# Expert feed-forward of a two-block transformer on one core: the four weight chunks of a group are loaded in reverse, and the group's matmuls are issued as one run

## The chip, the cores and the metric

The kernel runs on one core of one Trainium2 chip. The metric is the device time of one execution in microseconds. Three runs of the kernel before took 2832.05, 2836.18 and 2837.74 us; their median is 2836.18 us.

## What is computed

The reference runs two transformer blocks after each other over 512 tokens of width 1024, with a context of 256 tokens beside them. The first block mixes tokens by retention, window attention and neighbourhood attention, and ends in a feed-forward with 16 experts. This is the part that the change touches (`expert_choice_ffn`): each expert chooses its 64 best tokens by the router's probabilities, and computes for them, in float32,

```python
h = silu(xe @ w_gate[e]) * (xe @ w_up[e])     # [64, 1024] x [1024, 1024], twice
y = (h @ w_down[e]) * prob[e]                 # [64, 1024] x [1024, 1024]
out = out.at[idx[e]].add(y)
```

The second block is two layers of latent attention, pooling and a gated linear attention. Its work on the context (`ctx2`) needs nothing of the first block, and so can run at the same time as the experts.

## The kernel before

The kernel is written as Python generators. Each yields an estimate of the time that it has just written down, and `weave(main, fill, ratio)` takes one piece of the main work and then as many pieces of the fill as that estimate buys. In the experts' stage the main work is `experts` and the fill is `ctx2` of the second block's first layer, with a ratio of 0.8. What is written so is then put in order, engine by engine, by a list scheduler: of the instructions that are ready by its own estimates it takes the one of the highest priority, which is by default the place in the text. The order that results is fixed when the kernel is built, and each engine runs its list in order.

The 16 experts are taken in 8 pairs `p`. One pair has 24 weight pieces of 256 rows, `chunk(p, i, h)` being one half of such a piece: 128 partitions by 1024 float32, 512 KB, into a buffer `we`, loaded by SP's queue (line 1296). The first 44 chunks go to 20 buffers of an early pool (`NEARLY`, `NPRE`), all later ones to 8 buffers (`s.nbig`). A `group` is four chunks, `e` in 0, 1 (the expert of the pair) by `h` in 0, 1. It makes eight matmuls (line 1306): in `h`, in `kk`, and then the two experts. The tokens of an expert (64 columns of `xe`, or of `hT`) are stationary, 512 weight columns stream, and expert 0 writes partitions 0 to 63 and expert 1 partitions 64 to 127 of one PSUM tile. So the two matmuls of an `e` pair use different column halves of the array. Two groups give one PSUM tile (`G`, `U` or `Yp`); `act` makes the gated product from `G` and `U` by ACT and DVE (lines 1337 to 1339), `hturn` transposes it (line 1345), `Yp` is scaled by ACT (line 1374) and added to the result in DRAM by POOL's indirect DMAs (line 1380). An expert pair has 12 groups, the stage 96.

The fill's projections load a 128x1024 piece of weights (`wr`, line 412, SP's queue too, two buffers), split it into a high and a low part (`wh` by ACT at line 395, `wl` by DVE at line 391, three buffers each), and make three matmuls for each product (lines 404, 405, 406). In the trace each float32 matmul of line 1306 appears as two records, so a group is 16 records and a pair of matmuls four.

Of the kernel before, what the change touches and what calls it, by code (L numbers as in the profile page):

```python
# [10 lines left out]
AF = mybir.ActivationFunctionType  # L11
ALU = mybir.AluOpType
# [305 lines left out]
class Kern:  # L318
# [967 lines left out]
    def experts(s):  # L1286
        nc = s.nc
        wx = s.d["wexp"]

        def chunk(p, i, h):  # L1290
            if s.pre:
                s.pre -= 1
                w = s.early.tile([128, 1024], F32, name=s.uid("we"), tag="early", bufs=NEARLY)
            else:
                w = s.big.tile([128, 1024], F32, name=s.uid("we"), tag="wbig", bufs=s.nbig)
            nc.sync.dma_start(w, wx[p, i][:, h * 1024:h * 1024 + 1024])
            return w

        def group(p, c0, stat, ps, kh):

            for h in range(2):
                ws = [chunk(p, c0 + e, h) for e in range(2)]
                for kk in range(2):
                    k = 4 * kh + 2 * h + kk
                    for e in range(2):
                        nc.tensor.matmul(ps[64 * e:64 * e + 64, :], stat[:, k, 64 * e:64 * e + 64],  # L1306
                                         ws[e][:, kk * 512:kk * 512 + 512], start=k == 0, stop=k == 7)

        def gather(p):
            xg = s.T(nm="xg", tag="u")  # L1310
            nc.gpsimd.indirect_dma_start(out=xg, out_offset=None, in_=s.h2d, in_offset=bass.IndirectOffsetOnAxis(
                ap=s.idx128[:, p:p + 1], axis=0))
            return xg

        def turn(xg):
            xe = s.T(nm="xe", tag="u").rearrange("p (k n) -> p k n", k=8)
            for g in range(2):
                pt = s.at()
                for j in range(4):
                    k = 4 * g + j  # L1320
                    nc.tensor.transpose(pt[:, j * 128:j * 128 + 128], xg[:, k * 128:k * 128 + 128], s.const("ident"))
                (nc.scalar.copy if g else nc.vector.tensor_copy)(
                    xe[:, 4 * g:4 * g + 4, :], pt.rearrange("p (j n) -> p j n", j=4))
            return xe

        xg = gather(0)
        xe = turn(xg)
        for p in range(8):
            if p < 7:
                xg = gather(p + 1)  # L1330
            hT = s.T(nm="hT", tag="u").rearrange("p (k n) -> p k n", k=8)
            eth = s.T(nm="eth", tag="u")
            hd = []

            def act(f, G, U):
                th = eth[:, f * 512:f * 512 + 512]
                nc.scalar.activation(th, G, AF.Tanh, scale=0.5)
                nc.vector.scalar_tensor_tensor(th, th, 1.0, G, ALU.add, ALU.mult)
                nc.vector.tensor_tensor(th, th, U, ALU.mult)
                hd.append(th)  # L1340

            def hturn(f):
                pt = s.at()
                for j in range(4):
                    nc.tensor.transpose(pt[:, j * 128:j * 128 + 128], hd[f][:, j * 128:j * 128 + 128], s.const("ident"))
                nc.scalar.copy(hT[:, 4 * f:4 * f + 4, :], pt.rearrange("p (j n) -> p j n", j=4))  # L1346

            for f in range(2):
                G = s.mm()
                for kh in range(2):  # L1350
                    group(p, 8 * f + 2 * kh, xe, G, kh)
                    yield 3.6
                U = s.mm()
                for kh in range(2):
                    group(p, 8 * f + 4 + 2 * kh, xe, U, kh)
                    yield 3.6
                act(f, G, U)
                if f == 1:
                    if p < 7:
                        xe = turn(xg)  # L1360
                    hturn(0)
                    yield 1.4
            if p == 7:
                s.sums()
            ye = s.T(nm="ye", tag="u") if p < 7 else s.T(F32R, "ye", "u")
            for o in range(2):
                Yp = s.mm()
                for kh in range(2):
                    if o == 0 and kh == 1:
                        hturn(1)  # L1370
                    group(p, 16 + 4 * o + 2 * kh, hT, Yp, kh)
                    yield 3.6
                yo = ye[:, o * 512:o * 512 + 512]
                nc.scalar.activation(yo, Yp, AF.Copy, scale=s.gate[:, p:p + 1])
                if p == 7:
                    yl = s.T(F32R, "yl", "pj5")
                    nc.vector.scalar_tensor_tensor(yl, Yp, s.gate[:, p:p + 1], yo.bitcast(F32), ALU.mult, ALU.subtract)
                    s.last += [(yo[:, j * 128:j * 128 + 128], yl[:, j * 128:j * 128 + 128]) for j in range(4)]
            for e in range(2 if p < 7 else 0):
                nc.gpsimd.indirect_dma_start(  # L1380
                    out=s.ffd, out_offset=bass.IndirectOffsetOnAxis(ap=s.idx64[0:64, 2 * p + e:2 * p + e + 1], axis=0),
                    in_=ye[64 * e:64 * e + 64, :], in_offset=None, compute_op=ALU.add)
# [728 lines left out]

PACE = (2, 2.5, 2.5)
NEARLY = 20
NPRE = 44
LATE = True
XF = 1.0, 1.0
# [26 lines left out]
def body(tc, d, out):  # L2143
    from contextlib import ExitStack
    with ExitStack() as ctx:
# [16 lines left out]
        fill = Fill()  # L2162
        k.nbig, k.pre = 8, NPRE
        big = ExitStack()
# [49 lines left out]
```

## Time and profile before

| | |
|---|---|
| median of three runs | 2836.18 us |
| the profiled execution, its own time | 2832.7 us |
| its span | 2830.9 us |
| TensorE, matmuls (PE) busy | 2691.5 us, 95% |
| TensorE, weight loads (PEld) busy | 1867.8 us, 66% |
| VectorE (DVE) busy | 1567.8 us, 55% |
| ScalarE (ACT) busy | 1230.2 us, 43% |
| GpSimd (POOL) busy | 159.9 us, 6% |
| HBM read and written | 484.06 MB and 48.76 MB |
| first to last matmul of the experts | 828.6 to 1581 us of the span |

The time outside the span is 2832.7 - 2830.9 = 1.8 us. The page gives for each engine its busy time, then the span in 40 slices of about 71 us. The experts' stage is slices 12 to 22 of these. A busy PE in these tables has an instruction in its pipeline; how fast matmuls follow each other is read from their start times in the timeline.

### The profile page before, as it was taken

Reading aid. Unit: us, or ns where it says so; the run is one execution under the profiler, and the core shown is the slowest. Engines: PE = TensorE matmul, PEld = TensorE weight load, DVE = VectorE, ACT = ScalarE, POOL = GpSimd, SP = SyncE. Lnnn points to the kernel's source line nnn. Section 1 sums busy time; section 2 is a strip of 40 time slices with the busy share of each in tenths; the row PEclk is TensorE's granted clock in tenths of the full one; section 3 lists DMA queues with packets and bytes.
Section 4 is the critical chain, followed back from the end, with each engine's and each line's share of the span. In section 5 each row is a group of like instructions: output and inputs, shape, how many; then the busy total and the mean of one; then the engine's idle time right before and its main releaser. Section 6 shows DMA issues by size and latency. Waiting matters only on the chain. (4 is left out here: it accounts for less than half of the span.)

```text
span 2830.9 us, 41837 instructions
## 1 busy us (share of the span) xinstructions
PE 2691.5 (95%) x16372; PEld 1867.8 (66%) x16372; DVE 1567.8 (55%) x2957; ACT 1230.2 (43%) x2159; POOL 159.9 (6%) x260
## 2 busy tenths in 40 slices
PE   6899999999969999999999899999999999999997
PEld 3676677887623555555555477778777677778776
DVE  3554676675442323455222556666876646666874
ACT  3333454453222224455222354455655545555652
POOL 1000001110001000000000100000010000000001
PEclk9999999999979999999999999999999999999999
DMA  8545424635789898888899632214264432214353
GB/s 291 172 171 186 144 82 173 205 112 195 264 332 353 300 339 292 312 295 290 319 336 323 223 123 86 78 43 142 87 203 143 129 127 71 76 38 139 112 174 117
DMA packets 167974, 537.68 MB, mean 190 GB/s; under 512 B 21272, under 2 KB 22376, under 8 KB 167776
## 3 DMA queue, kind: packets, MB, share of 16 engines
q1 hardware_dynamic: 138528, 460.40, 46.6%
q0 software_dynamic: 17152, 52.57, 5.8%
q10 hardware_dynamic: 12096, 22.03, 2.1%
q8 instruction: 129, 2.11, 0.3%
q14 instruction: 69, 0.57, 0.1%
HBM read 484.06 MB, written 48.76 MB: 188 GB/s over the span
## 5 line engine op out<-in xcount | busy, mean ns | idle before, releaser
L391 DVE TENSOR_TENSOR wl<-wr,wh 128x1024 fp32r<-128x1024 f32 x320 | 390.7, 1222 | 358.4 <-ACT wh L395 340.4
L395 ACT CAST wh<-wr 128x1024 fp32r<-128x1024 f32 x320 | 334.1, 1046 | 417.5 <-PE ps L405 324.4
L404 PE MATMUL ps<-hx,wh 128*128 128x512 f32 x1168 | 473.2, 406 | 6.2 <-ACT hx L569 5.5
L405 PE MATMUL ps<-hx,wh 128*128 128x512 f32 x1168 | 468.4, 401 | 0.1
L406 PE MATMUL ps<-hx,wl 128*128 128x512 f32 x1168 | 466.1, 399 | 0.0
L1306 PE MATMUL ps<-we,xe 128*64 128x512 f32 x1024 | 293.5, 609 | 5.5 <-DMA we<-in_wexp 5.0
L404 PEld LDWEIGHTS ps<-hx,wh 128*128 128x128 f32 x1168 | 221.8, 190 | 66.2 <-issue 12.4
L405 PEld LDWEIGHTS ps<-hx,wh 128*128 128x128 f32 x1168 | 221.4, 190 | 51.5 <-issue 8.0
L406 PEld LDWEIGHTS ps<-hx,wl 128*128 128x128 f32 x1168 | 221.3, 189 | 50.0 <-issue 5.0
L673 ACT ACTIVATE P<-ps,st 128x768 f32<-128x768 f32 (+3 forms) x144 | 111.2, 772 | 143.4 <-DVE st L669 108.5
L1306 PEld LDWEIGHTS ps<-we,xe 128*64 128x64 f32 x1024 | 77.9, 137 | 134.1 <-issue 107.1
L404 PE MATMUL ps<-hc,wh 128*128 128x256 f32 x496 | 145.2, 294 | 3.6 <-ACT wh L395 3.4
L406 PE MATMUL ps<-hc,wl 128*128 128x256 f32 x496 | 144.2, 291 | 0.2 <-DVE wl L391 0.2
L1306 PE MATMUL ps<-we,hT 128*64 128x512 f32 x512 | 139.4, 601 | 3.0 <-ACT hT L1346 1.6
L405 PE MATMUL ps<-hc,wh 128*128 128x256 f32 x496 | 140.5, 284 | 0.0
L667 DVE TENSOR_REDUCE st<-ps 128x1 f32<-128x768 f32 (+3 forms) x144 | 114.1, 792 | 41.5 <-PE ps L406 39.0
L695 PE MATMUL ps<-c_ident,P 128*128 128x128 f32 x688 | 109.4, 278 | 5.3 <-ACT PT L698 3.6
L406 PEld LDWEIGHTS ps<-hc,wl 128*128 128x128 f32 x496 | 94.4, 190 | 28.3 <-issue 13.8
L404 PEld LDWEIGHTS ps<-hc,wh 128*128 128x128 f32 x496 | 94.5, 191 | 27.2 <-issue 15.1
L695 PEld LDWEIGHTS ps<-c_ident,P 128*128 128x128 f32 x688 | 79.8, 140 | 40.0 <-ACT PT L698 13.4
L698 ACT COPY PT<-ps 128x512 f32<-128x512 f32 x123 | 70.2, 587 | 77.4 <-PE ps L695 76.7
L471 PE MATMUL ps<-wm,sc_cc 128*32 128x512 f32 x384 | 87.7, 639 | 14.9 <-DMA wm<-in_wmod 14.6
(516 smaller groups left out, 5035.7 us busy)
## 6 DMA issues: line engine op xcount, KB each, us to landing
we<-in_wexp SPq DMA_DIRECT2D x384, 512.0 KB, 7.3
wr<-in_win SPq DMA_DIRECT2D x240, 512.0 KB, 3.9
wm<-in_wmod SPq DMA_DIRECT2D x48, 512.0 KB, 6.4
wr<-in_wbr SPq DMA_DIRECT2D x48, 512.0 KB, 4.4
dram<-th ACTq DMA_DIRECT2D x72, 256.0 KB, 2.2
mth<-dram SPq DMA_DIRECT2D x72, 256.0 KB, 3.1
wr<-in_wout SPq DMA_DIRECT2D x32, 512.0 KB, 3.6
dram<-mth POOLq DMA_DIRECT2D x48, 256.0 KB, 3.1
```

The source lines that it names most:

```text
L391: s.nc.vector.tensor_tensor(out, a, b, ALU.subtract)
L395: i = s.nc.scalar.copy(hi, src)
L404: t.matmul(out, a[0], b[0], start=start, stop=False)
L405: t.matmul(out, a[0], b[1], start=False, stop=False)
L406: t.matmul(out, a[1], b[0], start=False, stop=stop)
L471: nc.tensor.matmul(ps[32 * j:32 * j + 32, :], sc[:, k, :], w[:, j % 2 * 512:j % 2 * 512 + 512], start=k == 0, stop=k == 7)
L667: nc.vector.tensor_reduce(st[:, 0:1], sc[:, :n], AX.X, ALU.max)
L673: nc.scalar.activation(p[:, :n], sc[:, :n], AF.Exp, bias=st[:, 1:2], scale=scale, accum_out=st[:, 2:3])
L695: nc.tensor.transpose(tp[:, j:j + 128], blocks[(i + j) // 128], s.const("ident"))
L698: nc.scalar.copy(parts[i // 512][:, :m], tp[:, :m])
L1306: nc.tensor.matmul(ps[64 * e:64 * e + 64, :], stat[:, k, 64 * e:64 * e + 64], ws[e][:, kk * 512:kk * 512 + 512], start=k == 0, stop=k == 7)
```

## The change

`group` loads all four chunks before it writes down its first matmul, in reverse of their use: first `h` = 1 with expert 1 and expert 0, then `h` = 0 with expert 1 and expert 0. The lists are turned round again, so that `ws[h][e]` is the chunk of before, and the order of the eight matmuls among themselves stays. The matmuls, and the three instructions of `act`, are put 600 places forward in priority (`URGE`); the loads are not.

```diff
         def group(p, c0, stat, ps, kh):
 
-            for h in range(2):
-                ws = [chunk(p, c0 + e, h) for e in range(2)]
-                for kk in range(2):
-                    k = 4 * kh + 2 * h + kk
-                    for e in range(2):
-                        nc.tensor.matmul(ps[64 * e:64 * e + 64, :], stat[:, k, 64 * e:64 * e + 64],
-                                         ws[e][:, kk * 512:kk * 512 + 512], start=k == 0, stop=k == 7)
+            ws = [[chunk(p, c0 + e, h) for e in (1, 0)][::-1] for h in (1, 0)][::-1]
+            with s.tc.high_priority(URGE):
+                for h in range(2):
+                    for kk in range(2):
+                        k = 4 * kh + 2 * h + kk
+                        for e in range(2):
+                            nc.tensor.matmul(ps[64 * e:64 * e + 64, :], stat[:, k, 64 * e:64 * e + 64],
+                                             ws[h][e][:, kk * 512:kk * 512 + 512], start=k == 0, stop=k == 7)
...
             def act(f, G, U):
                 th = eth[:, f * 512:f * 512 + 512]
-                nc.scalar.activation(th, G, AF.Tanh, scale=0.5)
-                nc.vector.scalar_tensor_tensor(th, th, 1.0, G, ALU.add, ALU.mult)
-                nc.vector.tensor_tensor(th, th, U, ALU.mult)
+                with s.tc.high_priority(URGE):
+                    nc.scalar.activation(th, G, AF.Tanh, scale=0.5)
+                    nc.vector.scalar_tensor_tensor(th, th, 1.0, G, ALU.add, ALU.mult)
+                    nc.vector.tensor_tensor(th, th, U, ALU.mult)
                 hd.append(th)
...
+URGE = 600
```

In the built program the change shows in TensorE's list. The number behind a tile's name is the order in which the tiles were written down. The first place is in the fourth pair of experts, where the gated linear attention of the fill (lines 1772, 1799 and 1909 of before) runs beside a group. Before:

```order
L1306 MATMUL ps_10535<-we_10536,xe_9930 64x512
L1772 MATMUL ps_10484<-c_cum,la_9911 64x128 x2
L1772 MATMUL ps_10484<-c_cum,la_9920 64x128 x2
L1306 MATMUL ps_10535<-we_10538,xe_9930 64x512
L1306 MATMUL ps_10535<-we_10536,xe_9930 64x512
L1306 MATMUL ps_10535<-we_10538,xe_9930 64x512
L1306 MATMUL ps_10535<-we_10544,xe_9930 64x512
L1799 MATMUL ps_10504<-ql_9957,kl_10500 32x32 x8
L1909 MATMUL ps_10519<-qx_10459,st_10365 128x128
L1306 MATMUL ps_10535<-we_10546,xe_9930 64x512
L1306 MATMUL ps_10535<-we_10544,xe_9930 64x512
L1306 MATMUL ps_10535<-we_10546,xe_9930 64x512
```

After the change the same group stands so (the matmul's line is now 1307, and line 1799 is 1801):

```order
L1801 MATMUL ps_10381<-ql_9951,kl_10377 32x32
L1307 MATMUL ps_10535<-we_10542,xe_9930 64x512
L1307 MATMUL ps_10535<-we_10540,xe_9930 64x512
L1307 MATMUL ps_10535<-we_10542,xe_9930 64x512
L1307 MATMUL ps_10535<-we_10540,xe_9930 64x512
L1307 MATMUL ps_10535<-we_10538,xe_9930 64x512
L1307 MATMUL ps_10535<-we_10536,xe_9930 64x512
L1307 MATMUL ps_10535<-we_10538,xe_9930 64x512
L1307 MATMUL ps_10535<-we_10536,xe_9930 64x512
L1801 MATMUL ps_10381<-ql_9951,kl_10377 32x32 x7
```

The first matmul of before stood alone, the pair of the third product was cut in two, and now all eight follow each other. The first of them reads the chunk that was written down, and is loaded, last.

The second place is a group of the third pair of experts beside a projection of the fill. Before, the first matmul stands 23 rows of the fill ahead of its partner in some groups, and 10 rows ahead here:

```order
L405 MATMUL ps_7997<-yp_7436,wh_7993 128x256
L1306 MATMUL ps_7974<-we_8010,xe_7561 64x512
L406 MATMUL ps_7997<-yp_7435,wl_7994 128x256
L404 MATMUL ps_7997<-yp_7554,wh_7993 128x256
L405 MATMUL ps_7997<-yp_7555,wh_7993 128x256
L406 MATMUL ps_7997<-yp_7554,wl_7994 128x256
L404 MATMUL ps_7997<-yp_7682,wh_7993 128x256
L405 MATMUL ps_7997<-yp_7683,wh_7993 128x256
L406 MATMUL ps_7997<-yp_7682,wl_7994 128x256
L404 MATMUL ps_7997<-yp_7812,wh_7993 128x256
L405 MATMUL ps_7997<-yp_7813,wh_7993 128x256
L406 MATMUL ps_7997<-yp_7812,wl_7994 128x256
```

Behind these rows come the other seven matmuls of the group. After the change the fill's rows stand together, and the group behind them in one piece:

```order
L404 MATMUL ps_7997<-yp_7812,wh_7993 128x256
L405 MATMUL ps_7997<-yp_7813,wh_7993 128x256
L406 MATMUL ps_7997<-yp_7812,wl_7994 128x256
L1322 MATMUL ps_8290<-c_ident,xg_7854 128x128
L1307 MATMUL ps_7974<-we_8016,xe_7561 64x512
L1307 MATMUL ps_7974<-we_8014,xe_7561 64x512
L1307 MATMUL ps_7974<-we_8016,xe_7561 64x512
L1307 MATMUL ps_7974<-we_8014,xe_7561 64x512
L1307 MATMUL ps_7974<-we_8012,xe_7561 64x512
L1307 MATMUL ps_7974<-we_8010,xe_7561 64x512
L1307 MATMUL ps_7974<-we_8012,xe_7561 64x512
L1307 MATMUL ps_7974<-we_8010,xe_7561 64x512
```

The group ends at the same place of TensorE's list as before, to a few rows: it is the early matmul that has moved back to the other seven. (Line 1322 is a transpose of the next pair's tokens, which has moved in here too.) SP's list keeps its order of `we` and `wr` loads but for two neighbours that change places in two spots; POOL's is the same.

## Rows read from the trace of the kernel before

**Rows 1.** The page: TensorE's busy tenths and granted clock, and bytes moved, in 40 slices.

```profile
PE   6899999999969999999999899999999999999997
...
PEclk9999999999979999999999999999999999999999
...
GB/s 291 172 171 186 144 82 173 205 112 195 264 332 353 300 339 292 312 295 290 319 336 323 223 123 86 78 43 142 87 203 143 129 127 71 76 38 139 112 174 117
```

**Rows 2.** Windows, all instructions: length, busy us per engine (count), PEclk, DMA share, GB/s.

```profile
828.50:874.80 46.30, 45.69 (x210) 16.01 (x209) 4.48 (x8) 5.23 (x10) 5.61 (x10) 0.95 0.89 338
874.80:919.30 44.50, 39.35 (x154) 15.17 (x151) 13.03 (x34) 12.18 (x23) 5.60 (x7) 1.00 0.95 342
919.30:1581.60 662.30, 640.52 (x3907) 356.42 (x3906) 243.16 (x527) 223.39 (x441) 34.25 (x37) 0.99 0.88 314
```

**Rows 3.** Windows, line 1306 alone: length, PE busy, PEld busy, PEclk, DMA share, GB/s.

```profile
874.80:919.30 44.50, 31.41 (x98) 8.07 (x95) 1.00 0.95 342
919.30:1581.60 662.30, 355.60 (x1248) 94.04 (x1248) 0.99 0.88 314
```

**Rows 4.** Timeline of PE from 1005 us: start, us, engine, line, operation, records, idle before.

```profile
1005.54 0.28 PE L405 MATMUL ps<-hc,wh 128*128 128x256 f32 x1
1005.66 0.28 PE L406 MATMUL ps<-hc,wl 128*128 128x256 f32 x1
1005.87 3.65 PE L1306 MATMUL ps<-we,xe 128*64 128x512 f32 x14
1009.45 0.39 PE L404 MATMUL ps<-yp,wh 128*128 128x256 f32 x1
1009.67 0.28 PE L405 MATMUL ps<-yp,wh 128*128 128x256 f32 x1
...
1011.30 1.07 PE L1306 MATMUL ps<-we,xe 128*64 128x512 f32 x2
1012.30 0.39 PE L406 MATMUL ps<-hc,wl 128*128 128x256 f32 x1
```

**Rows 5.** Timeline of PE: other lengths of run, from 1315, 1318 and 1402 us.

```profile
1315.01 1.08 PE L1306 MATMUL ps<-we,xe 128*64 128x512 f32 x4
...
1318.19 1.94 PE L1306 MATMUL ps<-we,xe 128*64 128x512 f32 x8
...
1402.33 3.65 PE L1306 MATMUL ps<-we,xe 128*64 128x512 f32 x16
```

**Rows 6.** Windows: the loads' rate under the most pressure (columns as in rows 2).

```profile
838.00:868.00 30.00, 29.39 (x146) 10.54 (x144) 3.35 (x5) 2.62 (x5) 1.55 (x2) 1.00 1.02 402
...
882.00:900.00 18.00, 14.35 (x48) 3.96 (x46) 7.30 (x20) 6.36 (x12) 2.65 (x3) 1.00 1.03 360
...
960.00:1000.00 40.00, 39.94 (x215) 21.14 (x213) 11.20 (x19) 8.61 (x13) 3.94 (x3) 1.00 1.01 377
```

**Rows 7.** Waits of PEld, 919.3 to 1581.6 us, then 874.8 to 919.3: us, times, longest.

```profile
PEld ps L404 <- ACT wh L395: 18.1, 17, 2.6
...
PEld ps L1306 <- DMA we<-in_wexp: 5.7, 9, 2.0
...
PEld ps L1306 <- DMA we<-in_wexp: 9.6, 10, 2.3
```

**Rows 8.** Waits of SP's queue, 874.8 to 1581.6 us: us, times, longest.

```profile
SPq L1296 <- PE ps L1306: 384.2, 234, 8.7
SPq L412 <- DVE wl L391: 88.3, 27, 9.6
```

**Rows 9.** DMA issues: KB, median us to landing; 919.3 to 1581.6 us, then 838 to 868.

```profile
we<-in_wexp SPq DMA_DIRECT2D x304, 512.0 KB, 7.0
wr<-in_win SPq DMA_DIRECT2D x48, 512.0 KB, 8.7
...
we<-in_wexp SPq DMA_DIRECT2D x20, 512.0 KB, 10.5
```

**Rows 10.** Timeline of SP's queue, then of PE, around one group near 1481 us.

```profile
1477.61 1.26 SPq L412 DMA_DIRECT2D wr<-in_win  x1
1481.01 2.89 SPq L1296 DMA_DIRECT2D we<-in_wexp  x4
...
1479.89 3.65 PE L1306 MATMUL ps<-we,hT 128*64 128x512 f32 x14
1485.25 0.39 PE L404 MATMUL ps<-hc,wh 128*128 128x256 f32 x1 [1.71 <-ACT wh L395]
...
1498.63 1.94 PE L1306 MATMUL ps<-we,xe 128*64 128x512 f32 x8
```

## The prediction, as it was made before the run

> **What bounds the kernel now.** I read the page's slices first. In the experts' stage, slices 12 to 22, two things are high at once: TensorE is busy at nine tenths in nearly every slice, with its clock granted at nine tenths or more in all but one of them, and the loads run at 290 to 353 GB/s, more than in any later slice [rows 1]. So either could set the pace. The windows cut the stage in three [rows 2]: up to 874.8 us the early pool is consumed; from there to 919.3 TensorE is busy 39.35 of 44.50 us with the DMA share at 0.95; then come 662.3 us in which TensorE is busy 640.5 (97%) at a DMA share of 0.88 and 314 GB/s.
>
> The waits tell the two last stretches apart. In the short one the weight loads of line 1306 waited for a chunk 10 times in 44.5 us, 9.6 us in all; in the long one 9 times in 662.3 us, 5.7 us in all [rows 7]. The other way round, SP's queue waited 234 times, 384.2 us in all, for a matmul of line 1306 to free a chunk's buffer [rows 8]. So the short stretch hangs on the loads and the long one on TensorE. An example of the slack: four chunks are issued from 1481.01 on, over 2.89 us, and the run of that group starts at 1498.63 [rows 10]; with a median landing of 7.0 us [rows 9] the last was there at about 1484 + 7 = 1491, some 7 us early.
>
> **What TensorE loses in the long stretch.** It holds 1248 records of line 1306, which is 624 matmuls or 78 groups, and they were busy 355.6 us [rows 3], 4.56 us a group. How long a group takes when it is left in one piece is in the timeline: 16 records take 3.65 us [rows 5]. But 14 records take 3.65 us as well, and 2 records take 1.07 us where 4 take 1.08 [rows 4, 5]. So a matmul without its partner in the other column half costs what the pair costs: a step of 0.86 us (8 records, two pairs, take 1.94 against 1.08 for one), and an entry of about 0.2. A group that stands as one and seven pays 1.07 + 3.65 instead of 3.65. In TensorE's list before there are 154 runs in this stretch, 58 of them one matmul and 41 of seven; after the change there are 75, 72 of eight and 3 of sixteen, and not one of odd length.
>
> **The sum, part by part.**
> - The runs: 78 groups at 3.65 us make 284.7 us, against 355.6. That takes 70.9 us off TensorE.
> - Their borders. The fill's matmuls follow each other at 0.12 us (1005.54, 1005.66), but the one behind a run takes 0.22 to its follower (1009.45, 1009.67) and the one ahead of a run 0.21 (1005.66, 1005.87), while the run's busy time reaches 0.07 into it (1005.87 + 3.65 against 1009.45) [rows 4]. That is 0.10 + 0.09 - 0.07 = 0.12 us a run, and 154 - 75 = 79 runs go: 9.5 us.
> - So TensorE's need falls by about 80 us, from 662.3 to 582.
> - The loads. The bytes stay: 662.3 us at 314 GB/s are 208 MB [rows 2]. They need 208/402 = 517 us at the rate of the best 30 us, 208/377 = 552 at that of 960 to 1000, 208/360 = 578 in 882 to 900 [rows 6], and 208/342 = 608 at that of the stretch that hung on the loads [rows 2]. The first three are under 582, the last is over it. I take 600 us for the stretch, a mean of 347 GB/s: two streams that need about the same wait for each other, and the rows that hold rates over 350 are short. That is a gain of 62 us.
> - What is late next. The fill waited 18.1 us for its cast weights, 17 times [rows 7], as in the 1.71 us at 1485.25: that `wr` was issued at 1477.61 [rows 10], and these loads take 8.7 us to land [rows 9]. They stand in SP's queue behind the same chunks. With faster groups the load has less time; I let these waits grow by 40%, 7 us. Bounds: 0, as SP's waits for buffers shorten with TensorE, and 18 more, a doubling.
> - Up to 919.3 us I count nothing. The first stretch is nearly all pairs already, and the second hangs on the loads; its 98 records were busy 31.4 us where 98/16 x 3.65 = 22.4 would do [rows 3], so up to 9 us could come, and as much could be lost, since a group there can no longer start on its first two chunks.
> - The tanh and the two products of `act` move by a few places on ACT and DVE, which are busy 223 and 243 of 662 us [rows 2]: nothing. The order of SP's and POOL's queues hardly changes: nothing. Behind 1581 us the lists are those of before, so the rest moves up as it is.
>
> Together -62 + 7 = -55 us. The profiled execution took 2832.7 us, so 2777.7; the median of the three runs lies 3.5 us above it. I say **2779 us**.
>
> **A rule beside the rows.** What decides between 582 and 608 us is the rate that the loads can hold; rows show 402 GB/s over 30 us and no more than 353 in a slice of 71 us [rows 1, 6]. The Trainium skill, "DMA: Bandwidth & Descriptors", section "Bandwidth", gives 425 GB/s for one core that streams with its neighbour idle, and about 358 GB/s for each of two that stream. By the 425 the stretch's loads would need 490 us, an estimate from that page, and TensorE alone would set the pace; the 402 of rows 6 goes that way, and no row shows such a rate for long. By the 358 it would be 581 us, no more than TensorE's need.
>
> **The rivals.**
> - *The loads never bind.* For it: 7 us of slack in the example, and 377 GB/s held over 40 us with TensorE busy all through [rows 6]. Against it: the fill's weights, which are late already. Then all 80 us come, and the time is 2832.7 - 80 = 2753 us. Chance 0.15. (The page's 425 would be this case.)
> - *The loads take over.* All four chunks must have landed before a group's first matmul, and the loads hold no more than in the slices of the stage. At 330 GB/s, between the 314 of the stretch and the 342 of the one ahead [rows 2], 208 MB need 630 us: 32 us less the 7 to 18 of the fill's waits, about 2815 us. For it: the 342 stood over 44.5 us in which the DMA share was 0.95 and TensorE waited. Chance 0.13.
> - *Slower: the buffers turn round too slowly.* Eight buffers are two groups. A chunk buffer is free at the earliest when its matmuls in the run are through, the last of the four 3.65 us behind the run's start; its load must land before the run two groups on. A group takes 662.3/78 = 8.49 us now, so two take 17.0, and from 17.0 - 3.7 = 13.3 us of landing on, the period grows past the old one. Before, the first matmul needed only the chunk that was loaded first; now it needs the last. Against it: the landing is 7.0 us in the median, and 10.5 with the queue at its fullest [rows 9], where the period could still fall to (3.7 + 10.5)/2 = 7.1 us. At 13.8 us the period would be 8.75, 78 x 0.26 = 20 us more: 2853 us. Chance 0.06.
> - *Nothing.* TensorE comes sooner to the end of each group, and waits there for the fill's weights or for what they wait for, with the same end. The lists of TensorE exclude that the change does not do what it says; but a gain that is given back would look like this: 2832 to 2837 us. Chance 0.05.
>
> **How the numbers follow.** The forecast has 0.61, with 2765 to 2800 as its own range. A measurement of this kernel can tell about 0.2%, 6 us, from no change. The cases that are faster by more are the forecast, the first and the second rival: 0.89. Same: 0.05. Slower: 0.06. The range runs from 2750, just under the first rival, to 2818, just over the second; what it leaves out is the two last rivals and the far ends.
>
> **What would show it.** In the profile after: the runs of line 1307 in the timeline are 16 records of 3.65 us, with no 2 and no 14 left; line 1307's busy time in what is now the long stretch falls to 285 to 295 us; the stretch has 345 GB/s or more and is some 600 us long; the waits of TensorE for chunks, 5.7 us, and for the cast weights, 18.1, both grow, the sum of the two staying under 50 us. The first is near certain. I am wrong on the sum if line 1307's busy time falls and the stretch does not follow: then the waits for chunks name the second or third rival, and those for `wh` the fourth. If the stretch falls to 585 us with the waits unchanged, it is the first rival.

## The result, and the profile after

Four runs of the changed kernel took 2778.62 to 2799.95 us, median 2796.49 us, against 2836.96 us for the kernel before beside them. The ratio is 0.9855, with a 95% interval of 0.983 to 0.9879. Four more runs, beside the first experiments, gave 2788.01 us and a ratio of 0.9832 (0.9801 to 0.9864). I had forecast 2779 us, within 2750 to 2818: the direction and the range held, and the gain is 40 us, 48 in the second four, where I had said 57.

The profiled execution took 2794.44 us with a span of 2792.6 us, 38.3 us less than the one before. The windows of all instructions, cut at the same matmuls as the three stretches of before (start, end, length, busy us and count of PE, PEld, DVE, ACT and POOL, PEclk, DMA share, GB/s), and the work behind the stage as a last row:

```profile
833.90:928.80 94.90, 78.46 (x360) 32.15 (x359) 17.53 (x40) 16.70 (x32) 12.69 (x16) 0.92 0.88 315
928.80:1536.40 607.60, 575.17 (x3910) 345.97 (x3909) 244.13 (x526) 224.95 (x440) 34.02 (x37) 0.98 0.95 345
1536.40:2792.60 1256.20, 1203.76 (x8054) 933.18 (x8054) 812.87 (x1421) 655.96 (x1097) 52.89 (x92) 0.98 0.34 111
```

Before, the same cuts gave, for the first two stretches together and for the end:

```profile
828.50:919.30 90.80, 85.04 (x361) 31.18 (x360) 17.51 (x42) 17.41 (x33) 11.21 (x16) 0.98 0.92 340
...
1581.60:2830.90 1249.30, 1199.77 (x8054) 930.75 (x8054) 812.44 (x1421) 656.47 (x1097) 52.92 (x92) 0.98 0.34 112
```

So the long stretch went from 662.3 us [rows 2] to 607.6, 54.7 us less, and three places gave some back: the stage began 5.3 us later (833.9 against 828.6), its first 18 groups took 4.1 us more (94.9 against 90.8), and what follows took 6.9 us more. 54.7 - 5.3 - 4.1 - 6.9 = 38.4 us, the 38.3 us between the two spans but for rounding. The first of the three is scatter: nothing ahead of the stage has changed, and the second profile of the changed kernel began its stage at 829.3 us.

The windows of the expert matmuls alone, in the long stretch (PE and PEld busy, PEclk, DMA share, GB/s):

```profile
928.80:1536.40 607.60, 294.17 (x1248) 87.76 (x1248) 0.98 0.95 345
```

In rows 3 the same 1248 records were busy 355.6 us. And the timeline of PE shows why: a transpose of the experts, one whole group, and the fill behind it.

```profile
1034.44 0.60 PE L1347 MATMUL ps<-c_ident,eth 128*128 128x128 f32 x4
1034.97 3.65 PE L1307 MATMUL ps<-we,hT 128*64 128x512 f32 x16
1038.55 0.39 PE L404 MATMUL ps<-hc,wh 128*128 128x256 f32 x1
1038.78 0.28 PE L405 MATMUL ps<-hc,wh 128*128 128x256 f32 x1
1038.90 0.28 PE L406 MATMUL ps<-hc,wl 128*128 128x256 f32 x1
```

The waits of the weight loads in the same stretch (us, times, longest) against rows 7:

```profile
PEld ps L1307 <- DMA we<-in_wexp: 13.4, 9, 3.7
PEld ps L1815 <- ACT qd L1782: 6.6, 3, 2.2
PEld ps L404 <- ACT wh L395: 5.9, 7, 1.0
```

The wait for chunks has grown from 5.7 us, the wait for the fill's cast weights has shrunk from 18.1, and a wait for `qd` is new. The timeline shows what the last one is, in the part where the fill runs its gated linear attention:

```profile
1231.12 3.65 PE L1307 MATMUL ps<-we,hT 128*64 128x512 f32 x16 [0.55 <-ACT hT L1348]
1234.71 0.33 PE L1801 MATMUL ps<-ql,kl 128*32 128x32 f32 x16
1234.97 0.66 PE L1774 MATMUL ps<-c_cum,la 128*64 128x128 f32 x8
1237.58 0.25 PE L1815 MATMUL ps<-qd,kd 128*32 128x32 f32 x2 [1.95 <-ACT qd L1782]
1237.76 2.81 PE L1307 MATMUL ps<-we,hT 128*64 128x512 f32 x6
```

A whole group stands ahead of the cumulative sums (line 1774), and TensorE has nothing behind them until ACT has copied `bs`, `rs` and `qd`. Behind the 1.95 us of idling stands another group. Its first six records, at which the row ends, take 2.81 us, where at the full clock four take 1.08 us and eight 1.94 [rows 5]; the whole group took 5.35 us instead of 3.65. The granted clock had fallen to the lower level, 1.2 GHz, and the window of 3.2 us has it at half (columns as above):

```profile
1237.80:1241.00 3.20, 3.20 (x9) 0.96 (x10) 2.25 (x7) 3.00 (x8) 0.00 (x0) 0.50 0.87 341
```

This does not follow each such gap. Of the three waits for `qd`, all of 1.95 us, those at 1237.58 and 1285.90 us were followed by the lower clock, and behind the one at 1262.47 it stayed at 1.00.

### The profile page after: what moved, and what is told of

It reads as the page before. It is cut to its first block, busy times and chain, and to the rows that moved or that the text cites. A ratio compares the mean times of both kernels' runs of the same rounds, so it can differ in the third digit from the quotient of the medians.

```text
span 2792.6 us, 41759 instructions
## 1 busy us (share of the span) xinstructions
PE 2625.3 (94%) x16372; PEld 1859.9 (67%) x16372; DVE 1569.8 (56%) x2957; ACT 1230.6 (44%) x2159; POOL 161.0 (6%) x260
## 5 line engine op out<-in xcount | busy, mean ns | idle before, releaser
L1307 PE MATMUL ps<-we,xe 128*64 128x512 f32 x1024 | 241.1, 615 | 18.1 <-DMA we<-in_wexp 18.0
L1307 PE MATMUL ps<-we,hT 128*64 128x512 f32 x512 | 122.8, 626 | 10.4 <-DMA we<-in_wexp 8.2
L404 PEld LDWEIGHTS ps<-hc,wh 128*128 128x128 f32 x496 | 94.1, 190 | 19.5 <-issue 14.2
L405 PEld LDWEIGHTS ps<-hc,wh 128*128 128x128 f32 x496 | 94.0, 190 | 4.0 <-issue 3.5
```

The costliest lines, as they stand in the source:

```text
L404: t.matmul(out, a[0], b[0], start=start, stop=False)
L405: t.matmul(out, a[0], b[1], start=False, stop=False)
```

## The experiments

All ratios are to runs of the kernel before on the same chip, whose medians were 2834.7 to 2837.1 us.

**The priority without the reversed loads.** The four loads still stand ahead of the group's matmuls, in the order of use.

```diff
-            ws = [[chunk(p, c0 + e, h) for e in (1, 0)][::-1] for h in (1, 0)][::-1]
+            ws = [[chunk(p, c0 + e, h) for e in range(2)] for h in range(2)]
```

> The change's priority alone: the four chunks are loaded in the order of their use, all ahead of the matmuls, and the priority stays. In TensorE's list the long stretch (78 groups) then has 225 runs of expert matmuls (93 of one matmul, 102 of three) and 414 steps of a pair's length, against 154 runs and 372 steps before and 75 runs and 312 steps after. Theory (what counts is whether the two matmuls of a pair stand together, at 0.86 us a step and 0.27 us a run with its borders): 42 x 0.86 + 71 x 0.27 = 55 us more work on TensorE than before, which was busy 97% there: 2875 to 2895 us. Rival (the priority brings the gain, as it lets the experts and their gating go ahead of the fill): 2800 to 2837 us.

2928.71 us, ratio 1.0319 (1.0302 to 1.0337): slower by more than the theory said, and the rival is out. Its windows, all instructions and then the expert matmuls:

```profile
921.80:1676.80 755.00, 716.73 (x3909) 372.84 (x3908) 243.03 (x527) 223.73 (x441) 33.71 (x37) 0.99 0.80 276
```

```profile
921.80:1676.80 755.00, 411.06 (x1248) 101.16 (x1247) 0.99 0.80 276
```

The expert matmuls took 411.1 - 355.6 = 55.5 us more. My 55 was to hold for these and their borders together, but the rest of TensorE's work took 20.7 us more as well (305.7 against 284.9), and TensorE was idle 38.3 us instead of 21.8. By its timeline most groups stand in runs of three matmuls and of one:

```profile
1040.42 1.93 PE L1307 MATMUL ps<-we,xe 128*64 128x512 f32 x6
...
1043.18 1.07 PE L1307 MATMUL ps<-we,xe 128*64 128x512 f32 x2
```

So a high priority alone does harm. I read the list so: each matmul goes as soon as the scheduler takes its own chunk to have landed, ahead of its partner's.

**The reversed loads without the priority.** The two `with s.tc.high_priority(URGE):` become `if True:`.

> The reversed loads alone, without any priority. The long stretch has 96 runs and 321 steps. Theory: 9 x 0.86 + 21 x 0.27 = 13 us more on TensorE than in the changed kernel, some of it beside waits for chunks: 2800 to 2810 us. Rival (the priority brings half the gain or more): 2815 us or more.

2784.81 us, ratio 0.9812 (0.9795 to 0.9828): at least as fast as the whole change. The priority brings nothing that can be measured; the 21 runs that it joins in the list cost nothing in time. In the profile the expert matmuls and the stretch were both a little longer than with it (302.04 us of 610.6), so that the theory's sign is there, and its size isn't. So the reversal does the work, and its list says how: the chunk that is used first is loaded last, and 67 of its 96 runs are groups of eight without any priority, where before there were 16 of 154. That all four loads stand ahead of the matmuls is not the cause by itself: a kernel with that alone, the chunks in the order of use and no priority, was built but not timed, and its list has the 154 runs of before in the long stretch, 58 of them one matmul and 41 of seven.

**The early chunks in the order of their use.** `group` takes the order of `range(2)` while `s.pre` is positive.

> The changed kernel, but the chunks of the early pool are loaded in the order of their use; runs in TensorE's list as in the changed kernel. In the profile after, groups 6 to 18 took 6 us longer than before, with waits of 4.1 us at 872 and 4.9 us at 891 for chunks. Theory (a group there waits for the chunk that it uses first and that was loaded last): these waits shrink, 2789 to 2793 us. Rival (that stretch hangs on the rate of the loads, or differs from run to run): no difference, 2793 to 2800 us.

2786.08 us, ratio 0.9815 (0.9799 to 0.9832), beside 2788.01 for the changed kernel: no difference that these runs can tell. The profiles show the mechanism small and the right way round. The waits for chunks in the first 18 groups, of the changed kernel and then of this one:

```profile
PE ps L1307 <- DMA we<-in_wexp: 14.4, 5, 5.1
```

```profile
PE ps L1308 <- DMA we<-in_wexp: 10.1, 4, 3.8
```

The 18 groups took 94.4 and 93.0 us. The other profiles go the same way: with the early chunks reversed the 18 groups took 94.4 to 97.5 us in six profiles (both of the changed kernel, the reversal alone, `qd` first, and the two other ratios of the fill), with these chunks in the order of use 90.8 to 93.0 in three.

**The changed kernel again.**

> The changed kernel once more, beside the three others on this chip: 2785 to 2800 us if its runs scatter as the first four did (2779 to 2800).

2788.01 us (2779.97 to 2799.54). Its runs scatter by 20 us, those of the kernel before by 3 to 14.

**The same runs with partners apart.**

```diff
-                for h in range(2):
-                    for kk in range(2):
-                        k = 4 * kh + 2 * h + kk
-                        for e in range(2):
+                for e in range(2):
+                    for h in range(2):
+                        for kk in range(2):
+                            k = 4 * kh + 2 * h + kk
```

> The changed kernel with the eight matmuls of a group in another order: the four of expert 0 and then the four of expert 1, so that two neighbours use the same column half but for one place in the middle. The list's runs stay runs of eight. Theory (two matmuls of one column half take a step each, two of different halves share one): a run takes 7 steps and an entry, 7 x 0.86 + 0.2 = 6.2 us instead of 3.65, 96 x 2.55 = 245 us more, of which some 30 us are waits for chunks that it covers: 3000 to 3040 us. Rival (the run's length comes of the matmuls themselves, not of pairs): 2780 to 2800 us.

2905.51 us in one run, some 109 to 117 more than the changed kernel: the rival is out, and the size is half of what I expected. The timeline of two groups:

```profile
1043.76 5.42 PE L1307 MATMUL ps<-we,xe 128*64 128x512 f32 x16
1049.11 0.39 PE L404 MATMUL ps<-yp,wh 128*128 128x256 f32 x1
...
1050.73 5.42 PE L1307 MATMUL ps<-we,xe 128*64 128x512 f32 x16
```

A run takes 5.42 us, not 6.2 and not 3.65: six steps, not seven. In the middle, where expert 0 gives way to expert 1, two matmuls of each find a partner. The weight loads of the first group show it; each matmul has two of them, and they come singly, then in twos, then singly again (the row of three has the last load of the third matmul and both of the fifth):

```profile
1045.10 0.14 PEld L1307 LDWEIGHTS ps<-we,xe 128*64 128x64 f32 x1 [0.29 <-issue]
1045.53 0.19 PEld L1307 LDWEIGHTS ps<-we,xe 128*64 128x64 f32 x3 [0.29 <-issue]
1045.96 0.19 PEld L1307 LDWEIGHTS ps<-we,xe 128*64 128x64 f32 x2 [0.24 <-issue]
1046.39 0.19 PEld L1307 LDWEIGHTS ps<-we,xe 128*64 128x64 f32 x2 [0.23 <-issue]
1046.88 0.14 PEld L1307 LDWEIGHTS ps<-we,xe 128*64 128x64 f32 x1 [0.29 <-DMA wr<-in_win]
```

With 1.77 us more for each of 96 groups that would be 170 us, of which the idle time of the kernel after took up a part: TensorE was busy 701.19 of 720.80 us here.

**Half of the bytes.**

```diff
-            nc.sync.dma_start(w, wx[p, i][:, h * 1024:h * 1024 + 1024])
+            nc.sync.dma_start(w[:, 0:512], wx[p, i][:, h * 1024:h * 1024 + 512])
...
-                                             ws[h][e][:, kk * 512:kk * 512 + 512], start=k == 0, stop=k == 7)
+                                             ws[h][e][:, 0:512], start=k == 0, stop=k == 7)
```

> The changed kernel, but each chunk's load brings only the first 512 of its 1024 columns, and both products of a chunk use these: half of the experts' weights are left out; the loads, buffers and matmuls are as many as before. The scheduler joins more groups (44 runs in the long stretch, 34 of them two groups), which takes some 31 x 0.27 = 8 us off TensorE. Theory (after the change the loads are the second bound, worth the 32 us in which TensorE was idle in the long stretch of 607.6 us, and the waits before it): the long stretch takes 570 to 580 us and the kernel 2735 to 2765 us. Rival (TensorE and the fill's own waits hold the stretch): 2780 us or more.

2786.26 us in one run: the rival's number. The window of the long stretch:

```profile
903.90:1535.40 631.50, 585.15 (x3954) 357.47 (x3954) 248.22 (x549) 229.09 (x451) 34.67 (x39) 0.95 0.64 205
```

The loads moved 205 GB/s, and their rate could not have held it, yet it was 24 us longer. But the scheduler, which counts on shorter loads, had put the groups two by two, and with them fewer places at which a chain of the fill is covered: TensorE idled 46 us, waiting for chunks (7.2), for `qd` (5.9), for `hT` (5.0) and for others, 2 to 4 us each, and its granted clock was 0.95. The first 18 groups, on the other hand, took 81.0 us against 94.9, with 6.0 us of waits for chunks against 14.2: there the loads do hold TensorE. So fewer bytes help at the stage's start, and by themselves not behind it. What they would give with the order unchanged isn't told by this run.

**Six buffers.** `k.nbig` is 6.

> The changed kernel with 6 chunk buffers instead of 8, one and a half groups. Theory (what my slower rival rests on: a group's last chunks can be issued only when the run before has freed buffers): the last two chunks of a group are issued 1.9 us behind the start of the run before and land 5 to 7 us later, so the period is 7 to 9 us against 7.8 now: 2810 to 2880 us, with waits for chunks over 40 us. Rival (only the rate of the loads counts): 2780 to 2800 us.

2919.24 us in one run, beyond the theory's range. The longest wait of PE in its long stretch, and the window:

```profile
PE ps L1307 <- DMA we<-in_wexp: 73.8, 47, 5.7
```

```profile
946.50:1667.90 721.40, 611.80 (x3906) 356.05 (x3904) 241.69 (x525) 223.84 (x440) 33.06 (x36) 0.93 0.86 291
```

The period is 721.4/78 = 9.25 us against 7.8. The waits, 73.8 us, are over 40 as expected; on top comes the clock, granted at 0.93, so that the same matmuls were busy 611.8 us instead of 575.2. My slower rival is a real mechanism, two buffers away.

**More fill beside the experts, and less.** `RATIO_E` is 1.0, then 0.75.

> The changed kernel with the ratio of the weave at 1.0 instead of 0.8, so that more of the fill stands beside the experts and less behind them; 58 runs in the long stretch instead of 75. Theory (TensorE waits in the stage because the loads are now as long as its work, and behind it there are no loads): the idle time of TensorE in the stage, 32 us in the long stretch, falls by half or more: 2765 to 2785 us. Rival (the idle time comes of the fill's chains, and goes with the fill): 2785 to 2800 us.

> The changed kernel with the ratio of the weave at 0.75 instead of 0.8: of some 309 us of the fill's matmuls, by their lengths, 295 stand in the stage and 14 behind it; at 1.0 the fill ran out three half pairs ahead of the stage's end. Theory (loads and TensorE are level at 0.8): the stage loses 14 us of TensorE's work and waits about as much more for chunks, with the clock's loss on top: 2788 to 2810 us. Rival (TensorE still sets the pace, and the fill left over covers the gaps at the stage's end, 3.6 and 1.8 us): 2772 to 2786 us.

At 1.0: 2862.6 us, ratio 1.0093 (1.0076 to 1.011), slower than before the change, and neither the theory nor the rival had it. The windows of its last two parts:

```profile
1200.00:1400.00 200.00, 179.61 (x1534) 115.47 (x1532) 97.67 (x232) 89.54 (x191) 4.91 (x4) 0.91 0.75 269
1400.00:1609.00 209.00, 164.93 (x805) 76.61 (x801) 38.83 (x64) 36.36 (x61) 12.52 (x16) 0.90 0.92 328
```

The fill runs out early, and the last 209 us are groups without cover: TensorE is busy 165 us at a clock of 0.90, and waits 37.8 us for chunks. More fill beside the experts it was not: behind the stage TensorE has 8054 records as in the changed kernel, so at 0.8 no fill was left there to take in, and the higher ratio only moves it forward within the stage. At 0.75: 2804.97 us, ratio 0.9894 (0.9875 to 0.9914), in the theory's range. The stretch, then the end:

```profile
925.50:1530.50 605.00, 566.05 (x3820) 338.84 (x3819) 234.64 (x505) 221.06 (x431) 34.02 (x37) 0.98 0.94 342
1530.50:2803.20 1272.70, 1213.07 (x8144) 943.39 (x8143) 823.02 (x1443) 661.53 (x1107) 52.89 (x92) 0.98 0.34 112
```

In this profile 9 us of TensorE's work were taken from the stretch (566.05 against 575.17), and it became 2.6 us shorter; the end became 16.5 us longer. So in the changed kernel TensorE no longer sets the pace of the long stretch alone. With much more work it is slower (partners apart), with a little less it is hardly faster.

**`qd` first.** In `pre` of the gated linear attention the copies to `qd` are written down ahead of the cumulative sums.

```diff
             X.update(kd=kd, bs=bs)
+            if outputs:
+                rs, qd = s.T(nm="rs", tag="gh"), s.T(nm="qd", tag="gh")
+                for r in (F, B):
+                    nc.scalar.copy(qd[r, :n], st["q"][hd // 2][b0:b0 + 64, :n])
+                X.update(qd=qd, rs=rs)
...
-                rs, qd = s.T(nm="rs", tag="gh"), s.T(nm="qd", tag="gh")
                 nc.scalar.copy(rs[F, 1:n], pc[F, 0:n - 1])
                 nc.scalar.copy(rs[B, :n], pc[B, :n])
-                for r in (F, B):
-                    nc.scalar.copy(qd[r, :n], st["q"][hd // 2][b0:b0 + 64, :n])
-                X.update(qd=qd, rs=rs)
```

> The changed kernel with one thing moved in the fill: the copies to qd, which need nothing of the cumulative sums, are written down ahead of these and of the copies to bs and rs. In the profile after, TensorE waited three times 1.95 us for qd in the long stretch, each behind a group's run that stands right ahead of that chain, and the granted clock fell to half behind each. Theory (joined runs no longer stand between a chain's steps, so the chain shows; and a gap costs its clock besides): the three gaps go, 5.9 us, and the half-clock time of the long stretch, 20.5 us, falls by 10 or so, which is 5 us more: 2776 to 2786 us. Rival (the next step of that chain is waited for instead): 2787 to 2798 us.

2786.41 us, ratio 0.9823 (0.9803 to 0.9843). The waits for `qd` are gone from the long stretch, and two others head its list (the waits of PE):

```profile
PE ps L1307 <- DMA we<-in_wexp: 15.2, 12, 4.7
PE ps L533 <- DVE rs L508: 2.9, 1, 2.9
```

In the changed kernel the first was 12.0 us. The stretch took 611.3 us, not less than 607.6, and its granted clock was 0.98 as before the move. The theory's gain in the stretch did not come. The time, between the two ranges, decides nothing, and the rival is right only in part: what the gaps gave, other waits took, but these are for chunks and in another part of the fill, not at the next step of that chain. The half clock that I expected behind each of the three gaps stood behind two. The part behind the stage, where the same code runs in the second block, took 1245.9 us against 1256.2 and 1256.0 in the two profiles of the changed kernel; the next two runs, which have `qd` first too, gave 1245.4 and 1255.3 there, so this is no gain that can be counted on.

> qd first and the early pool's chunks in the order of their use, together, as the best version that the runs point to. Early chunks in order took 2 us off the first 18 groups and 4 us off their waits in the one profile: 2773 to 2785 us, under qd first alone by 0 to 4 us. Rival (that was the scatter of the runs): the same as qd first alone.

> The best version so far (reversed loads but for the early pool, qd first) without any priority: 96 runs in the long stretch instead of 75. The reversed loads alone were as fast as the whole change, though TensorE's list has 13 us more work by its runs. Theory (the few single matmuls and pairs that are left apart stand where a chain of the fill would wait, and cost little there): 2775 to 2786 us, as with the priority. Rival (13 us more on TensorE show once the other waits are gone): 2787 to 2796 us.

With both, 2781.47 us, ratio 0.9811 (0.9793 to 0.9829), and without the priority 2782.68 us, ratio 0.9807 (0.9787 to 0.9828). These are the lowest medians, 54 and 52 us under the kernel before and clear of it. Both lie in their theories' ranges, but against `qd` first alone (0.9823) and the reversal alone (0.9812) they differ by less than the intervals, so the rival of the first, no gain over `qd` first, is not out. The rival of the second, 2787 us or more, is.

## Why the prediction held, point by point

- **The cost of a lone matmul** was right, and is the cause of the gain. Three runs show it: the changed kernel, where 1248 records fall from 355.6 to 294.2 us; the priority alone, where they rise to 411.1 (414 steps of 0.86 us and 225 entries of 0.2 make 401); and the partners set apart, where the runs stay whole and still take 5.42 us. Of the 70.9 us I saw 61.4. The 9.5 us that are missing are groups at the lower clock, as the one at 1237.76: five groups of the long stretch took 5.2 to 5.9 us instead of 3.65, 8.9 us together.
- **The borders** were put at 9.5 us. The rest of TensorE's work in the stretch fell from 284.9 to 281.0 us, 3.9. That includes what the clock cost it. The Trainium skill, "TensorEngine Tiling (Array Packing)", section "Key Properties", says that a change of the tiling mode drains TensorE; a change from a run to the fill costs 0.23 us to the next start (1038.55 to 1038.78) where 0.12 is usual, which agrees, without showing the drain.
- **The long stretch** came out as forecast, -54.7 for -55, at 345 GB/s for the 347 that I took. That it came out so closely is luck in part. TensorE's busy time fell by 65.3 us (640.52 to 575.17), not by 80, and its idle time grew by 10.6, from 21.8 to 32.4, where the sum gave back 25, 18 for the loads and 7 for the fill's weights: two errors of 15 us that cancel. What TensorE waited for was another thing too. The fill's cast weights were to be later by 7 us; they were waited for 5.9 us instead of 18.1. In their place came 7.7 us more for chunks, 6.6 for `qd`, and the lower clock behind some of the gaps. That the loads would hold TensorE back is half shown: less work made the stretch hardly shorter, but half the bytes did not shorten it either, in another order. What sets its pace in the changed kernel stays open between the loads and the fill's chains; the profile shows both, in turn.
- **Where the gain is missing.** Not all groups gained alike. The 18 groups beside projections went from 155.4 to 133.1 us, 1.24 us each; the 12 groups beside the gated linear attention from 105.1 to 100.5, 0.38 each (windows of before, then of after):

```profile
972.30:1127.70 155.40, 148.04 (x784) 83.01 (x783) 41.23 (x66) 43.73 (x73) 7.59 (x8) 0.98 0.90 319
1227.30:1332.40 105.10, 103.13 (x1013) 54.55 (x1012) 68.07 (x205) 67.44 (x165) 3.51 (x3) 1.00 0.83 287
```

```profile
975.00:1108.10 133.10, 129.51 (x798) 80.10 (x800) 43.86 (x74) 45.18 (x77) 6.71 (x7) 1.00 1.00 370
1205.90:1306.40 100.50, 89.63 (x940) 50.54 (x936) 64.26 (x193) 62.38 (x155) 3.48 (x3) 0.93 0.87 298
```

  In the second pair TensorE was busy 13.5 us less, 8.5 of them with the experts' matmuls, and idled 8.9 us more: the fill's short chains, which the scattered matmuls used to cover, lie open (TensorE waited 0.2 us for `qd` there before, 5.9 after). The windows hold the same groups but not quite the same fill, 1013 records before and 940 after. With the six groups behind them, where 1302 and 1292 records stand, it is 156.5 and 151.3 us, 0.29 us a group, so the finding stays.
- **The steps that were mis-sized** besides are terms put at nothing. One is "up to 919.3 us I count nothing". The first 18 groups lost 4.1 us, inside the 9 that I had allowed. The reason that I had given, that a group can no longer start on its first two chunks, is a part of it: of waits of 14.2 us for chunks some 4 went when the early chunks were loaded in the order of use, and the rest stayed. Behind 1581 us "the rest moves up as it is" was short by 6.9 us in this profile and by 6.7 in the second; with the same lists there other profiles had 1252.5 and 1257.1 us (the reversal alone; early chunks in order), and before it was 1249.3. Three kernels whose edits lie in the stage alone (half the bytes, six buffers, partners apart) had 1248.7 to 1249.6 there, and wherever this part has these matmuls it took 1245.4 to 1257.1 us. So the 6.9 us are of the size of its scatter; what it scatters by is open. These two, and the later start of the stage in the one execution, are the difference between the forecast and the 38.4 us of the profile. My 2779 is also 2 us under my own sum: 2777.7 and the 3.5 us up to the median are 2781.
- **The rivals.** The loads never bind, 2753 us: did not happen, and no experiment reached it. The loads take over, about 2815 us: did not happen, the stretch took 607.6 us at 345 GB/s where that rival had 630 at 330. Slower for lack of buffers: not with eight, but with six. Nothing, 2832 us or more: out, as the intervals lie clear of 1.

## What to carry to other kernels

Where two narrow matmuls share the array by column halves, look at the order in which they stand, not only at their number: a matmul without its partner takes as long as the pair, and the busy time of a run of seven equals that of eight. A list scheduler that sends each instruction as soon as its operand has landed pulled such pairs apart here, and a higher priority made it worse; to let the first one need the operand that arrives last tied the group together without a word to the scheduler. What such scattered matmuls covered then lies open, so count on giving back a part: here the long stretch kept 55 of the 80 us that the sum had promised.

## What the runs showed of the hardware that I had not expected

Partners need not be neighbours: with four matmuls of one column half and then four of the other, a run took 5.42 us, six steps of 0.86, so two matmuls of each half still ran beside each other across the seam. The fifth matmul of the list started at 1045.54 us, with the third (1045.53) and ahead of the fourth (1046.39): matmuls of different column halves did not keep the list's order among themselves. And a gap can cost more than its length. With idle time of 109.6 us in the long stretch (six buffers) the granted clock was 0.93, and the same expert and fill matmuls were busy 611.8 us instead of 575.2.
